# A weighted sum of cached values on TensorE in place of GpSimd and VectorE

## The chip, the cores and the metric

The kernel runs on one core of a Trainium2 chip. The core has a matrix engine (TensorE, PE in the profile; its weight loads stand apart as PEld), a vector engine (VectorE, DVE), an activation engine (ScalarE, ACT), a general engine (GpSimd, POOL) and a queue engine that issues most transfers (SyncE, SP). The metric is the time of one execution on the device, in microseconds (us).

## The reference, cut to what matters

The program is one step of a two-layer decoder, for a prompt of 1024 positions and for eight sample rows (one new position each, with 1024 cached positions in 8 pages of 128). Layer 0 has forgetting attention with 8 heads of 64; of the samples it computes

```python
past = gather_pages(past_kv, page_table)
k_all = jnp.concatenate([past[:, :, 0], k], axis=1)
v_all = jnp.concatenate([past[:, :, 1], v], axis=1)
...
s = jnp.einsum('bqhd,bkhd->bhqk', q, k).astype(jnp.float32) * (HEAD_DIM ** -0.5)
s = s + (jnp.swapaxes(cq, 1, 2)[..., :, None] - jnp.swapaxes(ck, 1, 2)[..., None, :])
...
p = jax.nn.softmax(s, axis=-1).astype(v.dtype)
return jnp.einsum('bhqk,bkhd->bqhd', p, v)
```

The last line, for the cached part of the samples, is what this case is about: for each sample b, head h and channel d, the sum over 1024 cached positions of a weight p[b, h, position] times a cached value v[position, h, d]. All of it is f32.

## The kernel before, in words

The kernel is written as a set of streams (Python generators): the dense projections and the rest of the trunk (`gen_main`), the prompt's attention in layer 0 (`gen_attn(fox_units())`), the samples' attention in layer 0 (`gen_fox_dec`), and others. A small driver runs them against each other in an assumed time, which sets the order in which the instructions are written down; a stream says with each `yield` how much of that time a step takes, and waits with `need(...)` for flags of other streams. A list scheduler then orders the instructions of each engine once more, by its own model of their durations, and chooses the buffers. Each engine runs its instructions strictly in that order. PE's order therefore interleaves dense projections, attention and the samples' work, and an instruction that waits on PE holds all behind it. So it is with the SP queue: a load whose buffer isn't free holds the loads and stores behind it.

Buffers come from a pool `U` of up to 22 tiles of 4 KB in each partition, a pool `V` of half that size, and eight PSUM banks. Loads of weights (`wraw`), of pages (`kp`, `vp`), of prompt rows (`xnat`) and many intermediate tiles (`ph`, `s`, `nat`) share `U`.

Dense projections are the three f32r products at L339 to L341 (weights and activations split in a high and a low part), 344 columns at a time. The prompt's attention has scores (L530, and L532 for the mask), a DVE instruction that adds the bias and takes a running minimum (L533), an exponential on ACT, PE transposes (L251, tile `t`), copies of these to SBUF on ACT or DVE (tile `ph`), and products with the values (L921, tile `o`). The copy `rx` (L914) and the `tm` instructions finish a block of 256 queries.

The samples' attention in `gen_fox_dec` first does the cached keys, 32 steps of two pages (loads `kp`), then the softmax weights. These are turned by PE into `PTd`, a tile of 128 positions by (page, sample, head). Then come 32 steps over the cached values. Step n belongs to sample n // 4 and to two of its eight pages. Each has three parts, which `page_pairs` calls: `load_v` issues two transfers of 256 KB (a page of 128 positions by 512 values each) to a tile `vp`, two steps ahead; `step_v` multiplies the tile on GpSimd by the weights, each spread over the 64 channels of its head; `lag_v`, one step later, adds the two pages to `accd` (128 by 512) on DVE. After a sample's fourth step, `sum_v` sums `accd` over the 128 partitions: four PE products, each with 128 columns of `accd` as weights and a column of ones (L1178, tile `b`), and one ACT copy of 4 values in each partition to `dec_o`. The rest of `gen_fox_dec` adds the new position and the softmax's divisor, and sets the flag `foxdec`, on which the output projection's last part (`d<-mah`) waits.

The helper `tt` (L218) is a DVE tensor_tensor, `gt` (L221) the same on GpSimd, `act` (L215) an ACT copy or function, `mm` a PE product, `bank` a PSUM bank. `late(i)` tells the scheduler to place an instruction no earlier than the last dense group written down so far; it adds no wait on the chip.

Of the kernel before, what the change touches and what calls it, by code (L numbers as in the profile page):

```python
# [8 lines left out]
F32 = mybir.dt.float32  # L9
# [105 lines left out]
class Driver:  # L115
# [5 lines left out]
    def spawn(self, gen):  # L121
        self.live.append(Stream(self.now, self.n, gen))
        self.n += 1
# [36 lines left out]
def build(tc, I, O, C):  # L160
    nc = tc.nc
    with ExitStack() as ctx:
# [9 lines left out]
        def carve(pool, size, tag, cap, shape, dt, name):  # L172

            b = 2 if dt == BF else 4
            tag, cap = TAGS.get((tag, name), (tag, cap))
            t = pool.tile([128, size // b], dt, tag=tag, name=name, bufs=cap)
            v = t[:, :int(np.prod(shape[1:]))]
            if len(shape) > 2:
                ax = "abcd"[:len(shape) - 1]
                v = v.rearrange("p (%s) -> p %s" % (" ".join(ax), " ".join(ax)), **dict(zip(ax, shape[1:])))  # L180
            return v
# [4 lines left out]
        def V(shape, dt=F32, name="v"):  # L186
            return carve(vp_, UB // 2, "v", NV, shape, dt, name)
# [4 lines left out]
        def bank(name="b"):  # L192
            tag, cap = PTAGS.get(name, PTAGS["b"])
            return pb.tile([128, 512], F32, tag=tag, name=name, bufs=cap)
# [4 lines left out]
        def small(area, shape, name, bufs=1, dt=F32):  # L199

            n = int(np.prod(shape[1:]))
            if name not in slots:
                slots[name] = [tops[area], 0]
                tops[area] += n * bufs
                assert tops[area] <= (SMALL[0] if area == "g" else SMALL[1]), (area, tops)
            o = slots[name]
            v = sml[:shape[0], o[0] + n * (o[1] % bufs):o[0] + n * (o[1] % bufs) + n]
            o[1] += 1
            if len(shape) > 2:
                ax = "abcd"[:len(shape) - 1]  # L210
                v = v.rearrange("p (%s) -> p %s" % (" ".join(ax), " ".join(ax)), **dict(zip(ax, shape[1:])))
            return v if dt == F32 else v.bitcast(dt)

        def act(out, in_, func=AF.Copy, **kw):
            return nc.scalar.activation(out=out, in_=in_, func=func, **kw)  # L215

        def tt(out, a, b, op):
            return nc.vector.tensor_tensor(out=out, in0=a, in1=b, op=op)  # L218

        def gt(out, a, b, op):  # L220
            return nc.gpsimd.tensor_tensor(out=out, in0=a, in1=b, op=op)  # L221
# [15 lines left out]
        mm = nc.tensor.matmul  # L237
        dense = [None]

        def late(i):  # L240

            if dense[0] is not None:
                tc.add_manual_dep(i.ins, dense[0], LATER, reason="order")
            return i

        dma = nc.sync.dma_start
        ADD, SUB, MUL, MAX = ALU.add, ALU.subtract, ALU.mult, ALU.max
# [12 lines left out]
        flags, need, spawn = DR.flags, DR.need, DR.spawn  # L260
# [108 lines left out]
        ones = small("g", [128, 128], "ones")  # L369
# [667 lines left out]
        dec_o = small("0", [128, 4, 8], "dec_o")  # L1037
# [18 lines left out]
        def gen_fox_dec():  # L1056
# [8 lines left out]
            p = bank()  # L1065
# [21 lines left out]
            pmm = bank()  # L1087
# [5 lines left out]
            p = bank()  # L1093
# [8 lines left out]
            sd = {}  # L1102
# [28 lines left out]
            for a in range(2):  # L1131
                p = bank()
# [9 lines left out]
            PT = V([128, 8, 8, 8], F32, "PTd")  # L1142
            p = bank()
# [12 lines left out]
                return vp  # L1156

            def step_v(n, vp):
                b, g = n // 4, 2 * (n % 4)
                gt(vp, vp, PT[:, g:g + 2, b].unsqueeze(3).to_broadcast([128, 2, 8, 64]), MUL)  # L1160

            def lag_v(n, vp):
                b, g = n // 4, 2 * (n % 4)
                vf = vp.rearrange("p e h d -> p e (h d)")
                if g == 0:
                    sd["acc"] = V([128, 512], F32, "accd")
                    tt(sd["acc"], vf[:, 0], vf[:, 1], ADD)
                else:
                    tt(sd["acc"], sd["acc"], vf[:, 0], ADD)
                    tt(sd["acc"], sd["acc"], vf[:, 1], ADD)  # L1170
                if g == 6:
                    spawn(sum_v(b, sd["acc"]))

            def sum_v(b, acc):
                yield 2500.0
                pmm = bank()
                for t in range(4):
                    mm(pmm[:, t:t + 1], lhsT=acc[:, t * 128:(t + 1) * 128], rhs=ones[:, 0:1], start=True, stop=True)  # L1178
                act(dec_o[:, :, b], pmm[:, 0:4])
                flags.add("dv%d" % b)  # L1180

            yield from page_pairs(load_v, step_v, lag_v)
            yield from need("kv0", "kv1", "kv2", "kv3")
            hm = V([128, 4, 64], F32, "hm")
# [10 lines left out]
            pmm = bank()  # L1195
# [19 lines left out]
            pmm = bank()  # L1215
# [1398 lines left out]
```

## Time and profile before

| | |
|---|---|
| time, median of 3 runs | 2883.48 us (2883.11 to 2884.93) |
| the profiled execution | 2877.05 us, span 2875.2 us |
| mean granted PE clock in it | 0.948 |
| PE busy | 2576.8 us (90%) |
| DVE busy | 2195.1 us (76%) |
| ACT busy | 1341.9 us (47%) |
| POOL busy | 1191.2 us (41%) |
| loads of `kp`, first and last issue | 116.3 and 235.9 us |
| loads of `vp`, first and last issue | 326.4 and 518.6 us |
| products at L1178, first and last start | 366.4 and 541.5 us |

Times inside a profile count from the start of its span. A row of a group names the line, the engine, the operation, the tile written and the tiles read, the shapes, and the count; behind it come busy time and mean duration, and behind the next bar the idle time just before these instructions and who ended it. In a row of waits, "PE r L251 <- DVE small L533: 9.9, 2, 6.1" says that PE stood idle ahead of its L251 instruction on tile r until DVE's L533 on tile small was done, 9.9 us in total, twice, 6.1 at the longest. In a row of a stretch, the columns are the stretch, its length, and for each engine the busy time with the count of instructions; then the granted PE clock (1.00 is full), the share of the transfer engines and their rate. A row of the timeline has the start, the duration, the engine, the instruction and how often it stands there in a row. A matmul's duration overlaps its successor's, so the cost of one is the spacing of their starts.

The 56 sums on `accd` took 658 ns at the least and 4864 at the most, the 32 products on `vp` 1892 to 2363 ns.

### The profile page before, as it was taken

The page shows a single profiled execution, that of the slowest core. Times are in us where ns is not written, and L with a number is a line of the kernel's source. Part 1 is how long each engine was busy: PE and PEld are TensorE (multiplying, and loading weights), DVE is VectorE, ACT ScalarE, POOL GpSimd, SP SyncE. Part 2 cuts the span into 40 slices and gives each one's busy share as a digit, 9 for nine tenths or more (in the row PEclk, how much of TensorE's full clock was granted, in tenths as well). Part 3 has the DMA queues.
Part 4 walks back from the last instruction along what each step waited for, and adds up shares of the span by engine and source line. Part 5 has one row for each costly group of instructions (what it writes and reads, how often), then busy time and mean ns, then how long its engine had stood idle before and what let it go on. Part 6 is the DMA issues. An engine that isn't in the chain of part 4 may idle for free.

```text
span 2875.2 us, 48325 instructions
## 1 busy us (share of the span) xinstructions
PE 2576.8 (90%) x17916; PEld 2406.7 (84%) x17916; DVE 2195.1 (76%) x4243; ACT 1341.9 (47%) x2824; POOL 1191.2 (41%) x916
## 2 busy tenths in 40 slices
PE   7988888989999888899888758999969999889998
PEld 6977878979999888899877744567969999788898
DVE  4467897787566999996468899998386565999995
ACT  4236656344343433333255567779244444433331
POOL 2375554242222676730544525033041121667740
PEclk9999899989999999999989868999989999999999
DMA  4854567203232422222353335210313232432221
GB/s 130 265 157 130 162 210 266 95 30 109 98 118 89 147 90 97 89 96 92 89 159 109 113 85 131 75 56 23 111 38 110 97 118 89 133 103 82 96 89 60
DMA packets 254400, 318.91 MB, mean 111 GB/s; under 512 B 23617, under 2 KB 198889, under 8 KB 253909
## 3 DMA queue, kind: packets, MB, share of 16 engines
q1 hardware_dynamic: 207492, 275.68, 29.7%
q10 hardware_dynamic: 39616, 19.93, 2.4%
q0 software_dynamic: 7056, 20.22, 2.4%
q8 instruction: 141, 2.31, 0.3%
q14 instruction: 95, 0.77, 0.1%
HBM read 230.00 MB, written 85.81 MB: 110 GB/s over the span
## 4 chain that ended last, share of the span: by engine, by line
PE 48%; DVE 23%; issue 4%; ACT 3%; DMA 1%; POOL 1%; SPq 0%; DVEq 0%; ACTq 0%; POOLq 0%
PE d L1489 10%; PE d L1491 10%; PE d L1490 10%; DVE zr L218 4%; PE d L341 3%; PE d L339 3%; PE d L340 3%; DVE xT L218 2%; DVE fdu L218 2%; PE s L530 2%; DVE fd L218 2%; PE o L2081 2%; PE t L251 1%; DVE x1a L218 1%; DVE tjk L1975 1%
## 5 line engine op out<-in xcount | busy, mean ns | idle before, releaser
L221 POOL TENSOR_TENSOR fraw<-fraw,small 128x1024 f32<-128x1024 f32 x64 | 142.0, 2227 | 424.4 <-DMA fraw<-in_ffn_w 193.9
L1489 PE MATMUL d<-xoph,fs 128*128 128x258 f32 x768 | 219.0, 285 | 5.9 <-ACT z L215 4.9
L218 DVE TENSOR_TENSOR xT<-xT,d 128x258 f32<-128x258 f32 (+1 forms) x472 | 186.7, 423 | 45.8 <-PE d L341 31.4
L1490 PE MATMUL d<-xoph,fs 128*128 128x258 f32 x768 | 218.8, 285 | 2.6 <-DVE xoph L218 2.6
L1491 PE MATMUL d<-xoph,fs 128*128 128x258 f32 x768 | 218.6, 285 | 2.4 <-DVE fs L218 2.4
L339 PE MATMUL d<-xh,whif 128*128 128x344 f32 (+1 forms) x616 | 202.8, 330 | 5.7 <-DVE small L226 2.4
L341 PE MATMUL d<-xh,wlof 128*128 128x344 f32 (+1 forms) x616 | 198.9, 327 | 6.6 <-DVE wlof L218 6.6
L340 PE MATMUL d<-xl,whif 128*128 128x344 f32 (+1 forms) x616 | 200.9, 326 | 0.0
L215 ACT ACTIVATE s<-s,small 128x128 f32<-128x128 f32 (+7 forms) x192 | 149.5, 781 | 69.5 <-DVE small L533 68.8
L339 PE MATMUL d<-xh,whi 128*128 128x344 f32 x504 | 170.9, 340 | 11.0 <-ACT whi L215 5.5
L341 PE MATMUL d<-xh,wlo 128*128 128x344 f32 x504 | 165.7, 332 | 11.8 <-DVE wlo L218 11.6
L340 PE MATMUL d<-xl,whi 128*128 128x344 f32 x504 | 167.8, 333 | 0.0
L221 POOL TENSOR_TENSOR zoph<-zr,zoph 128x516 fp32r<-128x516 f32 x104 | 156.9, 1522 | 25.5 <-ACT zoph L215 24.6
L1489 PE MATMUL d<-xop,fl 128*128 128x258 f32 x512 | 147.9, 289 | 14.6 <-ACT fl L215 14.6
L1489 PEld LDWEIGHTS d<-xoph,fs 128*128 128x128 f32 x768 | 146.2, 190 | 7.0 <-ACT z L215 5.7
L1491 PEld LDWEIGHTS d<-xoph,fs 128*128 128x128 f32 x768 | 146.7, 191 | 2.9 <-DVE fs L218 2.8
L251 PE MATMUL t<-small,s 128*128 128x128 f32 x864 | 139.8, 280 | 10.4 <-DVE tm L218 3.0
L1490 PEld LDWEIGHTS d<-xoph,fs 128*128 128x128 f32 x768 | 146.4, 191 | 3.2 <-DVE xoph L218 3.2
L1491 PE MATMUL d<-xop,fl 128*128 128x258 f32 x512 | 146.7, 288 | 2.5 <-DVE fl L218 2.5
L1490 PE MATMUL d<-xop,fl 128*128 128x258 f32 x512 | 147.1, 287 | 0.0
L1489 PE MATMUL d<-zoph,fdu 128*128 128x258 f32 x448 | 133.1, 298 | 13.6 <-DVE xT L218 8.4
L221 POOL TENSOR_TENSOR zop<-zr,zop 128x516 fp32r<-128x516 f32 x78 | 117.2, 1512 | 63.4 <-ACT zop L215 36.9
(482 smaller groups left out, 9850.2 us busy)
## 6 DMA issues: line engine op xcount, KB each, us to landing
fraw<-in_ffn_w SPq DMA_DIRECT2D x120, 512.0 KB
d_z<-z SPq DMA_DIRECT2D x64, 516.0 KB
zr<-d_z SPq DMA_DIRECT2D x56, 516.0 KB
kp<-in_cache_fox_kv SPq DMA_DIRECT2D x64, 256.0 KB
vp<-in_cache_fox_kv SPq DMA_DIRECT2D x64, 256.0 KB
q1b<-d_q ACTq DMA_DIRECT2D x32, 512.0 KB
wraw<-in_ab_w_in SPq DMA_DIRECT2D x21, 512.0 KB
wrawf<-in_c_w_in SPq DMA_DIRECT2D x17, 512.0 KB
```

The costliest lines, as they stand in the source:

```text
L215: return nc.scalar.activation(out=out, in_=in_, func=func, **kw)
L218: return nc.vector.tensor_tensor(out=out, in0=a, in1=b, op=op)
L221: return nc.gpsimd.tensor_tensor(out=out, in0=a, in1=b, op=op)
L251: return nc.tensor.transpose(out, in_, ident[:n, :n])
L339: mm(ps, lhsT=wh, rhs=ah, start=(j == 0), stop=False)
L340: mm(ps, lhsT=wh, rhs=al, start=False, stop=False)
L341: i = mm(ps, lhsT=wl, rhs=ah, start=False, stop=(j == last))
L530: mm(p[:, :m], lhsT=lh[x], rhs=ks[:, k0:k0 + m], start=(x == 0), stop=(x == 1 and not dg))
L1489: mm(o, lhsT=wh[:, k], rhs=hi[:, cols], start=(start and k == 0), stop=False, skip_group_check=not start)
L1490: mm(o, lhsT=wh[:, k], rhs=lo[:, cols], start=False, stop=False, skip_group_check=not start)
L1491: i = mm(o, lhsT=wl[:, k], rhs=hi[:, cols], start=False, stop=(k == nk - 1), skip_group_check=not start)
L2081: mm(po[:64], lhsT=VF[g // 2][:, kb, 64 * (g % 2):64 * (g % 2) + 64], rhs=ph, start=(kb == 0), stop=(kb == i))
```

## The change

The product with the weights and the sum over positions become one operation on PE. For each page, the 128 positions by 128 values of two heads are taken as weights of a PE product, and the two heads' softmax weights (two columns of `PTd`) as the moving operand. The result, 128 (two heads by 64 channels) by 2, holds for each head's channels the right sum in one of the two columns and a product with the other head's weights in the other. Four such products cover a page, and 8 pages accumulate in the same 8 columns of a PSUM bank `va`, which a sample holds through its four steps. `lag_v` is empty. `sum_v` reads the right column for each half of the partitions: two ACT copies of 4 values by 64 partitions.

```diff
             def step_v(n, vp):
+
                 b, g = n // 4, 2 * (n % 4)
-                gt(vp, vp, PT[:, g:g + 2, b].unsqueeze(3).to_broadcast([128, 2, 8, 64]), MUL)
+                if g == 0:
+                    sd["acc"] = bank("va")
+                po = sd["acc"][:, :8].rearrange("p (t e) -> p t e", t=4)
+                for e in range(2):
+                    for t in range(4):
+                        i = mm(po[:, t], lhsT=vp[:, e, 2 * t:2 * t + 2].rearrange("p h d -> p (h d)"),
+                               rhs=PT[:, g + e, b, 2 * t:2 * t + 2], start=(g + e + t == 0), stop=(g + e == 7),
+                               skip_group_check=True)
+                        if e + t == 0:
+                            late(i)
+                if g == 6:
+                    spawn(sum_v(b, po))
 
             def lag_v(n, vp):
-                b, g = n // 4, 2 * (n % 4)
-                vf = vp.rearrange("p e h d -> p e (h d)")
-                if g == 0:
-                    sd["acc"] = V([128, 512], F32, "accd")
-                    tt(sd["acc"], vf[:, 0], vf[:, 1], ADD)
-                else:
-                    tt(sd["acc"], sd["acc"], vf[:, 0], ADD)
-                    tt(sd["acc"], sd["acc"], vf[:, 1], ADD)
-                if g == 6:
-                    spawn(sum_v(b, sd["acc"]))
-
-            def sum_v(b, acc):
+                pass
+
+            def sum_v(b, po):
                 yield 2500.0
-                pmm = bank()
-                for t in range(4):
-                    mm(pmm[:, t:t + 1], lhsT=acc[:, t * 128:(t + 1) * 128], rhs=ones[:, 0:1], start=True, stop=True)
-                act(dec_o[:, :, b], pmm[:, 0:4])
+                for e in range(2):
+                    es = slice(e * 64, (e + 1) * 64)
+                    act(dec_o[es, :, b], po[es, :, e])
                 flags.add("dv%d" % b)
```

Since the scheduler orders all instructions anew, the orders of the engines differ in more places than these. On PE they are the same up to the first of the value steps, differ through these steps, are the same through the feed-forward part of layer 0, and differ again in the attention of layer 1, where no instruction is added or removed. The loads of `vp` stay where they were in SP's queue but for a few that change places with stores.

## The prediction

> **What bounds the kernel now.** I read the page first: busy shares, then the chain of work that ended last.
>
> ```profile
> PE 2576.8 (90%) x17916; PEld 2406.7 (84%) x17916; DVE 2195.1 (76%) x4243; ACT 1341.9 (47%) x2824; POOL 1191.2 (41%) x916
> PE 48%; DVE 23%; issue 4%; ACT 3%; DMA 1%; POOL 1%; SPq 0%; DVEq 0%; ACTq 0%; POOLq 0%
> ```
>
> TensorE (PE) is busy 90% and holds half of the chain, GpSimd (POOL) 1% of it. An average over stages says little, so the second view is the one by stretches. The weighted sum runs from 326 us (first load of vp) to about 545 us (last product on accd).
>
> ```profile
> core 0: us, PE busy (x) PEld busy (x) DVE busy (x) ACT busy (x) POOL busy (x), PEclk, DMA share, GB/s
> 326.00:545.00 219.00, 193.96 (x1341) 181.49 (x1340) 183.41 (x356) 125.21 (x294) 107.41 (x91) 0.95 0.66 218
> 545.00:600.00 55.00, 55.00 (x415) 54.65 (x414) 31.29 (x60) 17.81 (x36) 10.88 (x12) 1.00 0.04 11
> ...
> 346.00:356.00 10.00, 4.57 (x22) 3.69 (x21) 9.78 (x18) 4.11 (x11) 2.58 (x4) 0.79 0.75 248
> 376.00:386.00 10.00, 10.00 (x73) 9.64 (x72) 7.84 (x21) 6.65 (x12) 0.00 (x0) 1.00 1.08 333
> 416.00:426.00 10.00, 5.61 (x41) 4.88 (x39) 9.55 (x11) 3.65 (x10) 6.97 (x5) 0.88 0.48 166
> 426.00:436.00 10.00, 8.10 (x37) 7.76 (x38) 6.35 (x14) 2.97 (x7) 1.02 (x1) 0.61 0.17 54
> ```
>
> In these 219 us PE is busy 194.0 and idle 25.0; VectorE (DVE) is busy 183.4. Where dense projections run (376 to 386), PE is full. Where it is not (346 to 356, 416 to 426), DVE is at 9.6 to 9.8 of 10. Behind the stage PE is full at once (55.00 of 55.00), so what the stage gains or loses in PE time is passed on: PE has a fixed amount to do, in a fixed order. The third view is what PE waited for in the stage.
>
> ```profile
> PE r L251 <- DVE small L533: 9.9, 2, 6.1
> PE o L921 <- DVE ph L218: 5.4, 7, 1.6
> PE b L251 <- DVE small L533: 2.5, 1, 2.5
> PE d L339 <- DVE tm L218: 1.5, 1, 1.5
> PE b L251 <- DVE ph L218: 1.5, 1, 1.5
> PE b L1178 <- ACT tm L215: 1.0, 1, 1.0
> PE o L921 <- DVE ks L218: 0.7, 1, 0.7
> ```
>
> Those that name DVE make 21.5 us. The timeline around the longest one shows who held DVE up:
>
> ```profile
> 427.90 0.69 PE L251 MATMUL r<-small,rx 128*128 128x128 f32 x2 [6.14 <-DVE small L533]
> ...
> 420.57 1.99 DVE L914 COPY rx<-small 128x256 f32<-128x256 f32 x1
> 422.48 2.38 DVE L218 TENSOR_TENSOR accd<-accd,vp 128x512 f32<-128x512 f32 x1
> 424.89 0.51 DVE L218 TENSOR_TENSOR ks<-d,ks 64x344 fp32r<-64x344 f32 x1
> 425.43 2.14 DVE L218 TENSOR_TENSOR accd<-accd,vp 128x512 f32<-128x512 f32 x1
> ...
> 420.06 4.26 POOL L221 TENSOR_TENSOR vp<-vp,PTd 128x1024 f32<-128x1024 f32 x2
> 425.12 1.90 POOL L221 TENSOR_TENSOR vp<-vp,PTd 128x1024 f32<-128x1024 f32 x1 [0.81 <-DMA vp<-in_cache_fox_kv]
> ```
>
> PE sits idle for 6.14 us while DVE does accd sums that take 2.1 to 2.4 us each, each beside a GpSimd product. So this stage has two limits: PE in the dense parts, and in the attention parts DVE, made slower by the very instructions that the change removes. The question is what PE pays for the relief.
>
> **The change, part by part.** Taken away:
>
> ```profile
> L221 POOL TENSOR_TENSOR vp<-vp,PTd 128x1024 f32<-128x1024 f32 x32 | 63.3, 1983 | 47.4 <-DMA vp<-in_cache_fox_kv 40.7 <-DVE accd L218 4.1 <-DVE ph L218 2.5
> L218 DVE TENSOR_TENSOR accd<-accd,vp 128x512 f32<-128x512 f32 x48 | 58.6, 1222 | 5.5 <-POOL vp L221 4.8
> L218 DVE TENSOR_TENSOR accd<-vp 128x512 f32<-128x512 f32 x8 | 10.8, 1352 | 2.4 <-PE r L251 2.0 <-POOL vp L221 0.4
> L914 DVE COPY rx<-small 128x256 f32<-128x256 f32 x13 | 9.7, 743 | 0.2
> L914 DVE COPY rx<-small 128x256 f32<-128x256 f32 x3 | 1.1, 369 | 0.1
> ```
>
> 63.3 us of POOL and 69.4 of DVE. The last two rows are the same copy in the stage and in the 70 us before it (256 to 326): 743 ns against 369, so with the GpSimd products gone the 13 copies should give back some 4.9 us more. DVE falls from 183.4 to about 109 us. POOL's 63.3 us are worth nothing by themselves: it holds 1% of the chain, and none of PE's waits quoted above names it.
>
> Added are 8 x 32 = 256 products on PE (one for each pair of heads, of each of two pages, in 32 steps), and the old 32 go. What one costs:
>
> ```profile
> L1178 PE MATMUL b<-small,accd 128*128 128x1 f32 x64 | 8.0, 242 | 1.0 <-ACT tm L215 1.0
> 366.37 1.05 PE L1178 MATMUL b<-small,accd 128*128 128x1 f32 x8 [0.97 <-ACT tm L215]
> 367.49 0.36 PE L921 MATMUL o<-ph,kv 128*128 128x256 f32 x1
> 1801.81 1.79 PE L2419 MATMUL do<-PT,kpg 128*128 128x64 f32 x15
> 539.42 0.62 PE L1197 MATMUL b<-small,qkx 128*64 128x1 f32 x8
> ```
>
> The 32 old products stand as 64 records: an f32 product is two passes. Eight passes take 1.05 us, one lasts 0.242, so they start (1.05 - 0.242)/7 = 0.115 us apart; with the way to the next instruction it is (367.49 - 366.37)/8 = 0.140 each. Layer 1's own product of cached values (64 columns wide, same 128x128 weights) takes at most 1.79/15 = 0.119 a pass. One column or 64 cost the same, so two will too. The new passes are 512, the old 64, the difference 448: 448 x 0.115 = **+51.5 us** of PE; bounds 448 x 0.140 = 62.7 above, and below, by the row with weights half as wide (0.62/8 = 0.078), 34.9. I take 0.115, since the new weights are 128x128.
>
> By the Trainium skill's page TensorEngine Tiling (Array Packing), section Instruction Overhead, a matmul has about 60 cycles of overhead, and one free column costs what 60 do. An estimate from that page alone, 60 cycles of 2.4 GHz = 0.025 us, would make the 448 passes 11 us and the change a gain (the second rival). The rows agree that columns don't count, but at 0.115, not 0.025.
>
> Where they stand: the scheduler puts them into the attention parts, between the attention products. On PE, at the head of the stage, before:
>
> ```order
> L530 MATMUL s<-kv,qst 128x256 x2
> L532 MATMUL s<-dmr 128x128
> L921 MATMUL o<-ph,kv 128x256 x5
> L530 MATMUL s<-kv,qst 128x384 x2
> L532 MATMUL s<-dmr 128x128
> L921 MATMUL o<-ph,kv 128x256
> L921 MATMUL o<-ph,kv 128x128 x2
> L530 MATMUL s<-kv,qst 128x512 x2
> L532 MATMUL s<-dmr 128x128
> L339 MATMUL d<-xh_100,whi 128x344
> ```
>
> and in the changed kernel:
>
> ```order
> L921 MATMUL o<-ph,kv 128x256
> L1166 MATMUL va<-PTd,vp 128x2 x8
> L921 MATMUL o<-ph,kv 128x256 x4
> L1166 MATMUL va<-PTd,vp 128x2
> L921 MATMUL o<-ph,kv 128x256
> L921 MATMUL o<-ph,kv 128x128 x2
> L1166 MATMUL va<-PTd,vp 128x2 x7
> L251 MATMUL r<-small,rx 128x128 x2
> L251 MATMUL t<-small,s 128x128 x4
> L1166 MATMUL va<-PTd,vp 128x2
> ```
>
> Three steps' products stand ahead of the next dense block, which before came right behind the scores. On DVE, the place of the 6.14 us wait (scores, copies rx and ks of the last attention tile), before:
>
> ```order
> L218 TENSOR_TENSOR accd<-vp 128x512
> L218 TENSOR_TENSOR accd<-accd,vp 128x512 x2
> L914 COPY rx<-small 128x256
> L218 TENSOR_TENSOR accd<-accd,vp 128x512
> L218 TENSOR_TENSOR ks_4028<-d,ks_4028 64x344
> L218 TENSOR_TENSOR accd<-accd,vp 128x512
> L533 ISA s,small<-s,bias,small 128x128
> ```
>
> and now:
>
> ```order
> L914 COPY rx<-small 128x256
> L533 ISA s,small<-s,bias 128x512
> L533 ISA small 128x1
> L218 TENSOR_TENSOR ks_4093<-d,ks_4093 64x344
> L533 ISA s,small<-s,bias,small 128x128
> L533 ISA small 128x1
> L218 TENSOR_TENSOR ph<-t,ph 128x512
> ```
>
> No sum stands ahead of the scores any more.
>
> *Idle of PE that goes.* The bounds are 0 and 25.0 us. In all but a few of the waits accd sums or stretched copies stand ahead of the instruction that is waited for; the rest are short hand-overs between PE and ACT or DVE that will stay. I take three quarters: **-19 us**. What is late next is PE itself.
>
> *Clock.* The mean granted clock of the stage is 0.95: at most 0.05 x 219 = 11 us. The three slices quoted with a low clock lose 4.57 x 0.21 + 5.61 x 0.12 + 8.10 x 0.39 = 4.8 us of busy time, and they lie at the long waits. I take **-6**. The Trainium skill (TensorE: Matmul & The Clock Gate, section HAM oscillation) wants no idle gap over about 3.4 us, since the clock then halves until PE has been busy for as long; for the one gap of 6.14 us and the other of some 3.8 (9.9 less 6.1) an estimate from it is 2 x 1.7 = 3.4 us, and the sum would be 2.6 us higher. The slice from 426 to 436, at 0.61 behind the gap, agrees with the rule's direction.
>
> *New waits.* A product now waits for its page on PE, in PE's order, and dense products are queued behind it, for which all else waits. POOL waited 40.7 us for the same transfers (12 times), with nothing better to do. That is the upper bound, 0 the lower. PE comes to each step later than POOL did, since each step adds 16 x 0.115 = 1.8 us ahead of the next. I take **+2**. Each pair of pages keeps its buffer until PE has read it, and SP's queue holds later loads until then; no term of its own, it lies in the same bound. ACT gets 16 small copies of 4 values in place of 8 (4 columns on half the partitions), 47% busy: nothing. One PSUM bank is held through four steps; the trace can't price that, it lies in the +2 and in the range.
>
> *Later.* The order also shifts in layer 1's attention with nothing added or removed. I take 0 and bounds of 8 us on either side, somewhat under half of the largest wait of PE in that part:
>
> ```profile
> PE b L2250 <- DVE small L226: 18.6, 5, 6.0
> ```
>
> Sum: +51.5 - 19 - 6 + 2 = **+28.5 us**. The profiled execution took 2877.05 (span 2875.2), 6.4 under the median of 2883.48; 2905.5 in its terms, **2912** in those of the median.
>
> **Rivals.**
>
> *PE waits for pages (more slower).* For: POOL's 40.7 us, and PE can't go round a waiting product. Against: PE's places for the products lie behind the attention products, late. With half of the 40.7 on PE, and only 10 us of idle and 3 of clock saved: 51.5 - 13 + 20 = +58.5, 2942.
>
> *PE's idle time pays for all (faster).* DVE sets the stage in the attention parts, and PE has room there. This needs cheap passes: the stage gains at most 25.0 + 11 = 36 us, so it decides at 36/448 = 0.080 us a pass, in every one of the 32 steps. The row with 64-column weights has 0.078; spacing alone, with some 0.2 us for the last pass, is (0.62 - 0.2)/7 = 0.060. At that: 26.9 - 36 = -9, 2874. Against: every row with 128x128 weights has at least 0.115. This is where the skill's 60 cycles would lead too.
>
> *No change.* All idle time and clock come back, a pass costs 0.100 (between the two kinds of rows), and the new order in layer 1 gives its 8 us: 44.8 - 36 - 8 = +1, 2884. For: PE's waits nearly all have a sum in front of them. Against: it takes three favourable ends at once.
>
> That the change doesn't do what it says is out: the order shows 256 products on PE and no product on vp on POOL.
>
> **How the numbers follow.** My forecast has 0.70, waiting for pages 0.13, the gain 0.08, no change 0.09. A difference under 0.2% (5.8 us) can't be told from none. Faster 0.08, same 0.09, slower 0.83. My forecast's own terms span +51.5 - 36 = +15 to 62.7 - 10 + 2 = +55. The range, 2889 to 2940, leaves out the gain, most of no change and the upper half of the waiting for pages.
>
> **What would show it.** In the stage: passes on va 512, about 0.24 us long, 0.115 apart (right), or under 0.08 (the gain). PE's waits for DVE down from 21.5 to under 6 us, the granted clock up from 0.95 to 0.98 or more. PE's waits that name the transfer of vp: some 2 us, or 20 (the first rival). The first product of the stage behind, which before starts here,
>
> ```profile
> L339 PE MATMUL d<-mah,whif x128: 277/283/293, 566.8 to 613.7; 128*128 128x258 f32 x128
> ```
>
> should start near 595. I am wrong if it starts before 575, or if it moves as said and the end of the kernel does not.

## The result, and the profile after

The changed kernel takes 2924.36 us (median of 4 runs, 2919.89 to 2933.25), the kernel before 2884.2 beside it (2883.11 to 2893.56). The ratio is 1.0139, with an interval of 1.0123 to 1.0155: slower, by 40 us. The forecast was 2912, its range 2889 to 2940.

The profiled execution of the changed kernel took 2933.25 us (span 2931.1) and is the longest of its four, that of the kernel before 2877.05. These two lie 56 us apart, more than the medians, so a second profile was taken of each, of the same programs on one chip: 2880.44 and 2921.18, 41 us apart. Both pairs are used below.

The page of the changed kernel, busy time and the chain that ended last:

```profile
PE 2645.4 (90%) x18364; PEld 2479.4 (85%) x18364; DVE 2157.3 (74%) x4187; ACT 1347.1 (46%) x2832; POOL 1124.9 (38%) x884
PE 58%; DVE 26%; issue 5%; ACT 5%; DMA 3%; POOL 2%; SPq 1%; another core or an unknown queue 0%; ACTq 0%; DVEq 0%; POOLq 0%
```

PE has 68.6 us more to do than before (2576.8), DVE 37.8 less and POOL 66.3 less. PE's share of the chain grew from 48% to 58%.

From here on "the stage" is the stretch from the copy that makes `PTd` to the first product on `mah`; both ends are the same instructions in every kernel. Its row by stretches (columns: the stretch, its length, busy time and count of PE, PEld, DVE, ACT and POOL, then the granted clock, the transfer share and GB/s), first before, in its two profiles:

```profile
326.10:566.80 240.70, 215.66 (x1479) 202.95 (x1478) 193.90 (x376) 129.40 (x299) 109.46 (x93) 0.96 0.61 200
```

```profile
324.30:563.20 238.90, 215.20 (x1480) 202.60 (x1479) 191.59 (x376) 130.29 (x299) 110.36 (x93) 0.96 0.62 202
```

and after, in its two:

```profile
329.80:601.30 271.50, 270.96 (x1927) 264.70 (x1926) 129.45 (x320) 134.02 (x308) 43.91 (x61) 0.92 0.55 178
```

```profile
329.00:600.30 271.30, 270.95 (x1927) 264.74 (x1926) 130.38 (x320) 134.19 (x308) 43.01 (x61) 0.92 0.55 178
```

The two profiles of a program agree within 2 us here. PE was idle for 25.0 of 240.7 us, and now for 0.5 of 271.5: it bounds the whole stage. DVE fell from 193.9 to 129.5, with the 56 sums gone. But the granted clock fell too, from 0.96 to 0.92, where it should have risen. Cut at the edges of the stretches in which the clock is at half (lows, for short), the changed stage shows where:

```profile
326.00:339.50 13.50, 13.42 (x114) 12.71 (x113) 7.77 (x24) 9.96 (x26) 4.90 (x3) 1.00 0.71 233
339.50:349.70 10.20, 10.20 (x44) 10.01 (x42) 4.25 (x8) 4.92 (x10) 6.27 (x5) 0.50 0.90 278
349.70:482.80 133.10, 132.65 (x1025) 129.63 (x1024) 63.55 (x162) 73.30 (x169) 22.01 (x36) 1.00 0.61 195
482.80:499.90 17.10, 17.10 (x79) 16.91 (x79) 5.22 (x17) 6.33 (x18) 0.96 (x2) 0.50 0.68 234
499.90:520.40 20.50, 20.49 (x169) 19.66 (x168) 11.53 (x28) 17.28 (x41) 5.43 (x7) 1.00 0.94 307
520.40:534.00 13.60, 13.60 (x59) 13.24 (x59) 2.84 (x7) 2.92 (x8) 1.45 (x2) 0.50 0.42 146
```

Three times the clock is at half, for 10.2 + 17.1 + 13.6 = 40.9 us together, and half of that, 20.5 us, is lost. PE is busy without a gap in each of them, and in the 6.8 us ahead of each it stands still for 0.45 us at the longest (its one wait for a page, at 481.8). Before, the lows lie at PE's gaps instead:

```profile
346.00:360.00 14.00, 8.57 (x45) 7.28 (x44) 12.27 (x25) 5.96 (x15) 5.24 (x11) 0.76 0.54 178
360.00:416.00 56.00, 51.81 (x355) 48.45 (x354) 49.52 (x98) 35.30 (x84) 29.90 (x25) 0.97 0.76 239
416.00:426.00 10.00, 5.61 (x41) 4.88 (x39) 9.55 (x11) 3.65 (x10) 6.97 (x5) 0.88 0.48 166
426.00:436.00 10.00, 8.10 (x37) 7.76 (x38) 6.35 (x14) 2.97 (x7) 1.02 (x1) 0.61 0.17 54
```

Length times what the clock lacks of 1: 3.4 + 1.7 + 1.2 + 3.9 = 10.2 us.

The group of the new passes and PE's waits in the changed stage (this is the only wait that the view names):

```profile
L1166 PE MATMUL va<-PTd,vp 128*128 128x2 f32 x512 | 67.8, 255 | 0.5 <-DMA vp<-in_cache_fox_kv 0.5
```

```profile
PE va L1166 <- DMA vp<-in_cache_fox_kv: 0.5, 1, 0.5
```

512 passes of about 0.25 us, of which a single one (at 481.8 us) waits for its page. The 21.5 us of waits for DVE are gone altogether. From start to next start the 512 passes take 59.4 us, 0.116 each, with the stretches at half clock in it; the median spacing is 0.112.

Taking the stage apart (the idle time and what the clock lost are taken off its length, what is left is PE's work at full clock):

| stage, us | before | after | difference | second pair | predicted |
|---|---|---|---|---|---|
| PE's work at full clock | 205.5 | 250.5 | +45.0 | 206.7, 250.4: +43.7 | +51.5 |
| PE idle | 25.0 | 0.5 | -24.5 | 23.7, 0.4: -23.3 | -19 and +2 |
| lost by the clock | 10.2 | 20.5 | +10.3 | 8.5, 20.5: +12.0 | -6 |
| length | 240.7 | 271.5 | +30.8 | 238.9, 271.3: +32.4 | +28.5 |

The rest of the 40 us lies outside the stage: it starts 3.7 us later (4.7 in the second pair), and from its end to the end of the kernel pass 2329.8 us for 2308.4 (in the second pair 2318.6 for 2315.4). Two profiles of one program differ there by 7 and by 11 us, so this part can't be read from one pair. DVE has 64.4 us less to do in the stage but 37.8 less in the whole kernel: it took longer behind the stage, above all up to layer 1's attention (896.8 us busy before, 924.1 after).

### The profile page after: what moved, and what is told of

It reads as the page before. It is cut to its first block, busy times and chain, and to the rows that moved or that the text cites. A ratio compares the mean times of both kernels' runs of the same rounds, so it can differ in the third digit from the quotient of the medians.

```text
span 2931.1 us, 49092 instructions
## 1 busy us (share of the span) xinstructions
PE 2645.4 (90%) x18364; PEld 2479.4 (85%) x18364; DVE 2157.3 (74%) x4187; ACT 1347.1 (46%) x2832; POOL 1124.9 (38%) x884
## 4 chain that ended last, share of the span: by engine, by line
PE 58%; DVE 26%; issue 5%; ACT 5%; DMA 3%; POOL 2%; SPq 1%; another core or an unknown queue 0%; ACTq 0%; DVEq 0%; POOLq 0%
PE d L1491 10%; PE d L1493 10%; PE d L1492 10%; PE d L339 5%; PE d L341 5%; PE d L340 5%; DVE zr L218 4%; PE s L530 3%; PE t L251 2%; DVE xT L218 2%; PE va L1166 2%; DVE fdu L218 2%; PE o L2083 2%; DVE fd L218 2%; PE o L921 1%
## 5 line engine op out<-in xcount | busy, mean ns | idle before, releaser
L341 PE MATMUL d<-xh,wlo 128*128 128x344 f32 x504 | 166.8, 334 | 15.8 <-DVE wlo L218 15.6
L218 DVE TENSOR_TENSOR zr<-zr 128x516 f32<-128x516 f32 x112 | 142.4, 1275 | 0.1
```

The source lines that it names most:

```text
L341: i = mm(ps, lhsT=wl, rhs=ah, start=False, stop=(j == last))
```

## The experiments

In what was expected, A is the theory that PE's work alone bounds the changed stage (passes at 0.10 to 0.115 us, and what the clock takes); the other letters are rivals, told where they stand. The rows are those of the stage, as above.

### A moving operand of 64 columns in place of 2

Each pass takes all 64 columns of `PTd` (8 samples by 8 heads) for its page. It uses two of the resulting columns; the rest is waste. Eight small ACT copies a sample read them instead of two.

```diff
-                po = sd["acc"][:, :8].rearrange("p (t e) -> p t e", t=4)
+                po = sd["acc"][:, :256].rearrange("p (t x) -> p t x", t=4)
...
-                               rhs=PT[:, g + e, b, 2 * t:2 * t + 2], start=(g + e + t == 0), stop=(g + e == 7),
+                               rhs=PT[:, g + e].rearrange("p b h -> p (b h)"), start=(g + e + t == 0), stop=(g + e == 7),
...
-                    act(dec_o[es, :, b], po[es, :, e])
+                    for t in range(4):
+                        c = 8 * b + 2 * t + e
+                        act(dec_o[es, t:t + 1, b], po[es, t, c:c + 1])
```

> The changed kernel with one thing different: the moving operand of each product on va is 64 columns wide (the weights of all samples and heads) in place of 2, and only the wanted columns are read afterwards, in 4-byte ACT copies (64 in all in place of 16). Count and order of the PE passes stay nearly the same. Theory A, the clock falls because passes with 2 columns leave the array nearly idle though PE is busy: the three stretches at half clock in the stage (41 us long, 20.5 us lost) are gone, a pass still takes about 0.115 us, and the time is 2904 to 2912, some 12 to 20 us under the changed kernel's 2924. Rival B, the clock's windows fall as they fall, whatever the columns: lows of 10 us and more stay in the stage and the time is 2920 to 2930. Rival C, wider passes cost more each: over 0.13 us a pass, 2930 or more.

Measured: 2904.86 us (2897.35 to 2907.05) beside 2885.16, ratio 1.0062 (1.0043 to 1.0081). 32 times the columns, and some 20 us less. Its stage and its group of passes:

```profile
326.70:579.40 252.70, 251.80 (x1927) 246.02 (x1926) 130.64 (x320) 136.44 (x355) 42.30 (x61) 1.00 0.58 191
```

```profile
L1166 PE MATMUL va<-PTd,vp 128*128 128x64 f32 x512 | 64.7, 270 | 0.3 <-DMA vp<-in_cache_fox_kv 0.3
```

The clock is at 1.00 through the whole stage. PE's work at full clock is 251.8 us, as with 2 columns (250.5). So a pass costs the same, and the 20.5 us that the changed kernel loses to the clock go with how narrow its passes are. Against the stage before, this one has 46.3 us more of PE's work, 24.1 less of idle time and 10.2 less lost by the clock, and is 12.0 us longer: with wide passes the clock does what the prediction wanted of it. The order of PE changed in a few places (175 of its 18364 rows stand otherwise); the two runs that follow bear on that.

### 16 columns

Eight samples by two heads as the moving operand. The instructions stand in the order of the changed kernel but for a few (62 of PE's 18364 rows, all of them in the stage).

```diff
-                po = sd["acc"][:, :8].rearrange("p (t e) -> p t e", t=4)
+                po = sd["acc"][:, :64].rearrange("p (t b e) -> p t b e", t=4, b=8)
...
-                               rhs=PT[:, g + e, b, 2 * t:2 * t + 2], start=(g + e + t == 0), stop=(g + e == 7),
+                               rhs=PT[:, g + e, :, 2 * t:2 * t + 2], start=(g + e + t == 0), stop=(g + e == 7),
...
-                    act(dec_o[es, :, b], po[es, :, e])
+                    act(dec_o[es, :, b], po[es, :, b, e])
```

> As the run with 64 columns, but with 16 (the two heads of all eight samples), in the changed kernel's order. If the clock goes by the share of time in which columns stream through the array, 16 of 64 is still little, and lows remain in the stage: 10 to 20 us lost there, 2914 to 2924. If a few columns suffice, none remain and the time is 2900 to 2908, as with 64.

Measured: 2913.41 us (2908.91 to 2922.37) beside 2881.93, ratio 1.0109 (1.0079 to 1.014).

```profile
326.30:597.70 271.40, 270.91 (x1928) 264.56 (x1927) 130.45 (x320) 133.93 (x307) 43.03 (x61) 0.92 0.54 178
```

The stage is that of 2 columns, within 0.1 us, with three lows at nearly the same places (335.3, 478.7 and 516.2 us, where the stage starts 3.5 us earlier) and 20.5 us lost in them. 16 columns don't help, 64 do. The median is 11 us under that of 2 columns, though the stage is the same: a first sign that times outside the stage wander by such amounts. (The kernel before was measured beside each; against that, it is 31.5 us slower here and 40.2 there.)

### Every product of 64 columns twice

This gives the price of a pass by itself. The sums come out doubled.

```diff
-                        i = mm(po[:, t], lhsT=vp[:, e, 2 * t:2 * t + 2].rearrange("p h d -> p (h d)"),
...
+                        for z in range(2):
+                            i = mm(po[:, t], lhsT=vp[:, e, 2 * t:2 * t + 2].rearrange("p h d -> p (h d)"),
```

> The kernel with 64 columns, each product on va done twice (1024 passes in place of 512), so that the weighted sums double. Theory A, PE sets the stage and a pass costs 0.115 us: the stage from the softmax weights to the first product on mah, 252.7 us with 64 columns, grows by 512 x 0.115 = 59, the time to 2958 to 2970. Rival, part of the passes still hides in PE's waits: under 2950.

Measured: 2960.91 us (2960.09 to 2963.74) beside 2881.93, ratio 1.0283 (1.0255 to 1.031).

```profile
326.80:634.80 308.00, 307.92 (x2439) 302.66 (x2438) 131.47 (x320) 138.37 (x355) 43.61 (x61) 1.00 0.49 157
```

512 passes more lengthen the stage by 308.0 - 252.7 = 55.3 us, at a clock of 1.00 in both and with PE full in both: 0.108 us a pass. Twice as many passes of 64 columns bring no low either. So it isn't the number of passes on this tile that brings the clock down.

### One product of four

Only the first of each page's four products; three quarters of the sums are left out. This takes away 384 passes and keeps everything else of the change.

```diff
-                    for t in range(4):
+                    for t in range(1):
...
-                    act(dec_o[es, :, b], po[es, :, e])
+                    act(dec_o[es, :, b], po[es, 0:1, e].to_broadcast([64, 4]))
```

> The changed kernel with three quarters of the products on va left out (one of four pairs of heads, 128 passes in place of 512), so the sample attention's sums are incomplete; loads, waits and ACT copies stay, GpSimd products and VectorE sums are gone as in the changed kernel. It shows what the relief alone is worth, with PE's price nearly taken away. Theory A, PE's idle time behind the VectorE sums was real and goes: 128 passes cost 14.7 us, the old 64 saved 7.4, and 20 to 30 us of idle and slow clock come back, so 2860 to 2872, faster than before. Rival, the relief is worth little since other waits take the place of those removed: 2884 or more.

Measured: 2870.97 us (2866.4 to 2875.82) beside 2885.16, ratio 0.9953 (0.9938 to 0.9968).

```profile
328.00:546.10 218.10, 213.58 (x1544) 206.10 (x1543) 125.29 (x320) 130.58 (x308) 42.80 (x61) 0.98 0.67 221
```

With 4.5 us idle and 3.4 lost by the clock, PE's work is 210.2 us; against the 250.5 of the changed kernel the 384 passes were worth 40.3, or 0.105 each. This kernel is 14 us faster than before: relieving DVE and POOL is worth something, and the passes, with what the clock takes, are what undoes it.

### GpSimd's products put back

The changed kernel, with the old product of each step done on GpSimd as well, into a tile that nobody reads. DVE's sums stay away.

```diff
+                if n == 0:
+                    sd["junk"] = U([128, 2, 8, 64], F32, "vj")
+                gt(sd["junk"], vp, PT[:, g:g + 2, b].unsqueeze(3).to_broadcast([128, 2, 8, 64]), MUL)
```

> The changed kernel with the 32 GpSimd products put back beside PE's products, written to a scratch tile that nobody reads. Theory A, the stage is now set by PE, and VectorE has room (100 of 219 us busy), so GpSimd's 63 us and what they slow on VectorE cost little: within 6 us of the changed kernel's 2924. Rival D, what held PE up before was above all VectorE instructions slowed by GpSimd's products: PE's idle time comes back in part, 2932 to 2945.

Measured: 2918.26 us (2913.62 to 2919.34) beside 2885.16, ratio 1.0115 (1.0098 to 1.0131).

```profile
322.30:595.00 272.70, 268.73 (x1928) 260.75 (x1927) 131.62 (x320) 133.69 (x308) 104.16 (x93) 0.94 0.54 177
```

60 us of GpSimd work more, and the stage is 1.2 us longer; PE's idle time grows from 0.5 to 4.0 us, and the clock takes 17.1 in place of 20.5. Once PE bounds the stage, and DVE has no sums to do, the GpSimd products cost nearly nothing. The rival by which they slow the changed kernel (2932 to 2945) falls.

### Half of the samples on PE

Samples 1, 3, 5 and 7 go the new way with 2 columns, the others the old way (the old code of `step_v`, `lag_v` and `sum_v` beside the new).

```diff
+            on_pe = (1, 3, 5, 7)
...
+                if b not in on_pe:
+                    gt(vp, vp, PT[:, g:g + 2, b].unsqueeze(3).to_broadcast([128, 2, 8, 64]), MUL)
+                    return
```

> Four of the eight samples (1, 3, 5, 7) use PE's narrow products, the other four the GpSimd products and VectorE sums of before. Theory A, PE's idle time of 25 us is a reserve that is used up first: 256 passes less 32 cost 25.8 us, most of the idle and slow clock goes with half of the sums, so between 2880 and 2896. Rival E, the price is a straight line in the number of narrow passes, without a reserve: half of the whole effect, 2904.

Measured: 2897.63 us (2890.8 to 2909.99) beside 2885.16, ratio 1.0036 (1.0021 to 1.005).

```profile
330.00:587.60 257.60, 250.77 (x1704) 241.55 (x1703) 156.75 (x348) 132.09 (x304) 74.88 (x77) 0.91 0.57 187
```

The median lies between the two expectations, nearer to that of A, and settles nothing. The profile (of its slowest run, 2909.99) shows both costs in one stage: 6.8 us of idle time and 22.2 lost by the clock.

### Two samples on PE, with 64 columns

As the last one, with the wide operand and samples 2 and 5 alone.

```diff
+            on_pe = (2, 5)
```

> Two of the eight samples (2 and 5) use PE's products with 64 columns, six the GpSimd products and VectorE sums of before. 128 passes less 16 old ones cost 12.9 us of PE, and if PE's idle time and slow clock behind the VectorE sums (25 and 10 us) go in proportion or better, 9 to 18 us come back: the stage is 236 to 245 us long, against 240.7 before. Layer 1 stands in the order that seems to cost 11 us, so 2886 to 2898 in all; with a stage under 236 the idle time goes first with few sums removed.

Measured: 2889.51 us (2886.63 to 2896.65) beside 2881.93, ratio 1.0037 (1.0023 to 1.005).

```profile
327.30:568.90 241.60, 226.63 (x1591) 217.05 (x1590) 177.56 (x362) 131.77 (x314) 92.12 (x85) 0.95 0.61 200
```

The stage is 0.9 us over that of before, within what was expected; the time is 7.6 us over, so most of that lies outside the stage. PE's work grows by 214.7 - 205.5 = 9.2 us, the idle time falls by 10.0 and the clock takes 1.7 more. PE's idle time just about pays for a quarter of the samples here.

### The kernel before, with 24 of the 56 sums on GpSimd

Nothing on PE changes. Of the seven sums on `accd` that a sample takes, three go from DVE to GpSimd: 24 of 56, and not the 28 (half) that the expectation below counts.

```diff
-                    tt(sd["acc"], sd["acc"], vf[:, 0], ADD)
+                    gt(sd["acc"], sd["acc"], vf[:, 0], ADD)
```

> The kernel before with 28 of the 56 sums on accd on GpSimd in place of VectorE, and nothing added to PE. If VectorE's queue is what held PE up, half of the sums off it should give back half of PE's idle time of 25 us in the stage and part of the slow clock: the stage 225 to 235 us against 240.7, the time 2868 to 2880, faster than both kernels. Rival: GpSimd's longer work (107 us busy in the stage, and some 36 more) slows VectorE's other instructions as much as the sums did, and no time is won: stage 238 or more, 2880 to 2892.

Measured: 2876.08 us (2870.29 to 2879.48, 10 runs) beside 2880.49 (13 runs), ratio 0.9983 (0.9971 to 0.9995). It is the one kernel here that does the whole work and has a lower median than both; at 0.17% it lies just under what was called measurable.

```profile
323.40:556.80 233.40, 212.01 (x1480) 200.18 (x1479) 173.55 (x352) 128.96 (x300) 138.01 (x117) 0.98 0.62 207
```

DVE loses 20 us of work, and PE's idle time falls only from 25.0 to 21.4. Of the 7.3 us that the stage is shorter, 5.1 are the clock's (5.1 lost in place of 10.2). The stage and the time came out as expected, but not by the idle time, of which half was to come back. PE's longest waits in this stage:

```profile
PE t L251 <- DVE tm L218: 5.7, 1, 5.7
PE o L921 <- DVE ph L218: 4.9, 4, 1.9
PE s L530 <- DVE small L533: 4.5, 4, 2.0
PE r L251 <- DVE small L533: 1.8, 1, 1.8
```

They still name DVE, which still has 32 of the 56 sums among its other work. And seven times DVE itself now stands still ahead of one of them until GpSimd is done with its own sum on the same `accd`, for 15.8 us in total.

### Layer 1's order, moved by another edit

The changed kernel has another order in layer 1's attention, with no instruction added there. In the first profiles that part took longer: PE's weight loads for the scores there (tile `q1b`), from the first start to the last, go from 1707.1 to 2006.0 before and from 1751.3 to 2062.2 after, 298.9 and 310.9 us. Here the kernel before has one assumed time changed, which gives layer 1 another order and keeps the way of the sums.

```diff
-                yield 2500.0
+                yield 1500.0
```

> The kernel before with one number different: the assumed delay ahead of the four products that sum up a sample is 1500 in place of 2500. Nothing is added or removed, but the scheduler then puts layer 1's attention nearly in the order that it has in the changed kernel (15 rows of PE differ from that, 290 from the kernel before). Theory F, that order costs about 11 us by itself, as the profiles say (first to last score with q1b 299.5 us before, 311.5 changed, 310.8 with 64 columns, 310.5 with a quarter of the products): the same span is 308 to 313 us and the time 2890 to 2898. Rival, the difference is chance of one execution: the span is 297 to 303 us and the time 2880 to 2888.

Measured: 2886.82 us (2879.72 to 2891.88, 10 runs) beside 2881.93 (19 runs), ratio 1.0022 (1.0006 to 1.0038). Its row of these loads (count, shortest, median and longest in ns, first and last start), then those of the second profiles of before and after:

```profile
L530 PEld LDWEIGHTS s<-ks,q1b x384: 186/190/351, 1708.1 to 2011.6; 128*128 128x128 f32 x192
```

```profile
L530 PEld LDWEIGHTS s<-ks,q1b x384: 186/190/351, 1705.2 to 2009.3; 128*128 128x128 f32 x192
```

```profile
L530 PEld LDWEIGHTS s<-ks,q1b x384: 186/190/351, 1747.3 to 2049.8; 128*128 128x128 f32 x192
```

303.5 us in the other order, just over the rival's range; 304.1 and 302.5 in the second profiles of before and after. So one and the same program differs by 5 to 8 us in this span, and the first pair's 12 us can't be put down to the order. That the order costs 11 us at every execution (F) isn't borne out: span and time both stay under its ranges. A smaller cost isn't ruled out. The time is 4.9 us above that of the kernel before, by the interval 1.7 to 11, though the stage is a little shorter (236.9 us); and the span was 310.2 with 64 columns, 309.8 with a quarter of the products and 308.9 with every product twice, but 304.1 with 16 columns and 298.6 with the GpSimd products put back.

### Second profiles of both kernels

> The kernel before once more, for a second profile of the same program: how far do the stage (240.7 us, 25.0 idle, 10.2 lost by the clock) and layer 1's span from the first to the last score with q1b (299.1 us) repeat? If the changed order of layer 1 costs time, this span stays at 297 to 301; if its difference was chance, it may come at 303 to 311.

> The changed kernel once more, for a second profile: the stage was 271.5 us with 0.5 idle and 20.5 lost by the clock, layer 1's span 311.1. If the lows come from the runs of narrow passes, they fall at the same places again (behind 339, 482 and 520 us) and 15 to 21 us are lost; if from chance, elsewhere or not at all. Layer 1's span is expected at 303 to 307, as in the run with 16 columns, whose order is the same.

Measured: 2880.44 and 2921.18 us. Their rows of the stage and of layer 1 stand above; the span after, 302.5 us, is just under what was expected. The stage repeats: its length within 2 us, the lows after at 337.8 to 348.0, 481.2 to 501.6 and 522.1 to 532.4. What follows it does not: from the first product on `mah` to the end 2315.4 us for the kernel before (2308.4 in the first), 2318.6 after (2329.8).

## Why the prediction was right, and where it was not

**What bounds the stage: right.** PE had a fixed amount of work, the relief was worth no more than what PE's idle time and slow clock held, and the price of the passes decided. PE's idle time after is 0.5 of 271.5 us, and 512 passes more on top lengthened the stage by 55.3 us, all on PE. The size of the relief was read a little high: 69.4 and 4.9 us were to go from DVE, and its busy time in the stage fell by 64.4. Durations that are added up overstate it, since they overlap: the copy at 420.57 us, 1.99 long, ends after the next sum's start at 422.48.

**Passes: right in kind, somewhat too dear.** +51.5 was forecast, +45 measured (+43.7 in the second pair), inside the bounds of 34.9 and 62.7. A pass costs 0.108 us at full clock, by the doubled kernel, and not 0.115. The old passes that go were worth more than the same price: by the row quoted there they cost 0.140 each with the way to the next instruction. 512 x 0.108 - 64 x 0.140 = 46.3. The reading that 2 columns cost what 64 cost held: PE's work at full clock is 250.5, 250.4 and 251.8 us with 2, 16 and 64.

**Idle time: nearly all of it goes.** Forecast -19 of 25.0, measured -24.5. The prediction had kept a quarter for short hand-overs between PE and ACT or DVE. They didn't stay: with PE full, the others have long done what it comes for. The page waits, +2, came to 0.5.

**Clock: the step that failed.** The prediction took -6, since the lows before lie at the long waits and those would go. The waits went, and the clock takes 10 us more than before. The step was wrong in its reading of what a low follows: not an idle PE alone. The trace shows 17.1 us at a clock of 0.50 in which PE was busy for 17.10, with 23 of the narrow passes in the 6.8 us ahead; 64 columns in the same passes, and the lows are gone. The Trainium skill (TensorE: Matmul & The Clock Gate, section HAM oscillation) speaks of idle gaps only; the lows at 339.5, 482.8 and 520.4, with no gap over 0.45 us in the 6.8 us ahead of them, aren't covered by it.

That the term came out at +10 in place of -6 was covered up, by luck, by three others that were too cautious in the other direction: 45 for 51.5, -24.5 for -19, 0.5 for 2. So the stage came to +30.8 for the +28.5 forecast.

**Later: 0 was taken, some 9 us are open.** Of the 40 us between the medians the stage holds 31 to 32. The stage starts 3.7 and 4.7 us later, though PE's order is the same up to it: in the nine other kernels it starts anywhere from 322.3 to 330.0. What follows the stage differed by 21 us in one pair and by 3 in the other. That layer 1's order costs 11 us each time wasn't borne out, a smaller cost stays possible. Whether the rest is a cost of the change or only wandering of long programs isn't settled by these runs. Against a fixed cost speaks the kernel of 16 columns, which has nearly the same order and the same stage and is only 31.5 us above the kernel before.

For a fixed cost speak the profiles taken together: from the stage's end to the kernel's, the four without any product on `va` take 2308.4 to 2316.1 us, the seven in which every sample has them 2316.9 to 2329.8, the two mixed ones 2316.0 and 2320.6. Of that, up to the first load of `q1b` (1140.3 and 1142.0 us before, 1150.0 and 1147.0 after), PE is idle as long as before (132 to 133 us), and the clock takes more (66.6 and 63.8 us before, 76.2 and 71.6 after). Why it does stays open.

**The rivals.** Waiting for pages is out: one wait of 0.5 us. That PE's idle time pays for all needed 0.080 us a pass; it is 0.108. No change needed a gain in the clock, and there was a loss.

The profile's own marks: the first product on `mah` was to start near 595 and started at 601.3,

```profile
L339 PE MATMUL d<-mah,whif x128: 277/282/292, 601.3 to 648.3; 128*128 128x258 f32 x128
```

PE's waits for DVE were to fall under 6 us and fell to none, the clock was to rise to 0.98 and fell to 0.92.

## What to carry to other kernels

When the profile shows an engine full behind a stage, an added piece of work can only be paid from what that engine idles, or loses to a slow clock, inside the stage: 25 and 10 us here, for 45 of passes. A small f32 product with full 128x128 weights costs the same with 2 columns as with 64 (0.108 us a pass here), so a sum over partitions with 2 useful columns is a dear one, and extra columns up to those 64 cost nothing. Where such products stand in runs, look at the granted clock with PE busy, not only at its gaps; widening the moving operand may be worth trying: it took 20 of the 40 us back here.

## What the runs showed of the hardware

That the clock can halve while PE is busy was not expected. In the search for what the lows have in common, the columns that PE streamed were counted from the trace's matmul records (start and shape) in the last 3.4 us ahead of each change of the clock, since the clock's records change on a grid of that length. In the 13 profiles, between 330 and 600 us, 33 lows begin. Ahead of 31 of them PE started 0.65 columns a nanosecond or fewer, ahead of the other two 0.70 and 0.75. Before, the figures are 0.28, 0.30 and 0.56 (gaps); after, 0.65, 0.57 and 0.18 (narrow passes). Of 905 such stretches at full clock that no low followed, 12 were at 0.70 or less (0.49 to 0.68). So gaps and narrow passes look like one thing: few columns in 3.4 us. It would explain why 16 columns changed nothing (0.56, 0.70 and 0.27) and why 64 did (never under 0.77); but with every product twice four stretches were at 0.62 to 0.68, and no low followed. This was counted afterwards, on these profiles. No run was made to test the limit, and the exceptions on both sides show that it isn't the whole rule.
